# The w_up products of a decoder layer in Strassen's form, in three passes of 688 tokens

## The chip, the cores and the metric

The kernel runs on one core of a Trainium2 chip. The metric is the device time of one execution in microseconds (us). The core has five engines that run their own instruction streams: TensorE (PE; its weight loads are listed as PEld), VectorE (DVE), ScalarE (ACT), GpSimd (POOL) and SyncE (SP), which issues most of the DMA transfers. SBUF is the working memory of 128 partitions, PSUM the memory that TensorE accumulates in, DRAM the memory off the core.

## The reference

One decoder layer on 2048 prompt tokens and 8 single-token samples, 2056 rows in all, of width 1024. Attention (dilated windows) and retention run side by side; their outputs go through `w_out`. The part that is changed follows:

```python
x1  = layernorm(ALPHA * x + mix, ln1_g, ln1_b)
h   = jnp.square(jax.nn.relu(jnp.einsum('btd,df->btf', x1, w_up)))   # 1024 -> 4096
ffn = jnp.einsum('btf,fd->btd', h, w_down)                           # 4096 -> 1024
y   = layernorm(ALPHA * x1 + ffn, ln2_g, ln2_b)
```

All inputs and outputs are float32.

## The kernel before

Every matrix product is made from two parts of each operand: a high part, rounded to the type that TensorE reads at full pace (`split`: ScalarE makes `h`, VectorE the rest `l = raw - h`), and three products, `wh*xh + wh*xl + wl*xh` (`gemm`, lines 244 to 246). One matmul takes a 128x128 block of weights and up to 512 columns of tokens. Activations lie with the model dimension on the partitions and the tokens along the columns.

The kernel has two halves. In the first, four quarters of 512 tokens go through the input projection, attention, retention and the output projection `w_out`; its `evac_out` writes `ALPHA*x + mix` to DRAM (`zd`). In the second, the feed-forward part (`ffn(s)`), two passes `s` take 1024 and 1032 tokens. A pass walks over 8 groups `g`. In a group, four tiles `f` of `w_up` (each 128 output columns, K = 1024 in 8 steps) give four tiles of the hidden layer: `up` accumulates 24 matmuls for each chunk of tokens in a PSUM bank (`ups`), ScalarE makes relu (`rl`) and its square's high part (`hid`), GpSimd the square in float32, VectorE the low part. Then four tiles of `w_down`, of 1024 columns, give eight outputs: `down` accumulates 12 matmuls per chunk (`dps`), and VectorE adds the bank to `ya`, which holds the pass's result in SBUF over all groups. Pass 0 uses two chunks of 512 tokens, pass 1 three of 344, the first and last groups other cuts (`w_keep` holds four weights and walks over chunks outside).

Weights come one at a time from `wseq` (`w_load`: 512 KB into `wr`, on SP; `w_split`: `wh`, `wl`, three buffers each). `fx` holds x1 of the pass, high and low parts.

LN1 is a stream of jobs (`ln_jobs`: sums, mean by a matmul with ones `lm`, centring, sum of squares, `lvv`, scale and shift), one for each chunk of 344 tokens, in slots that own temporaries. `tick(pe)` advances a planned time as products are emitted and emits jobs of the streams whose engines are planned to be free within 4 us; `flush` emits the rest of them without products between. The compiler's list scheduler then sets each engine's order from priorities (program order) and readiness. LN1 of pass 0 starts while `w_out` of the last quarters still runs; the first group of pass 0 takes its first chunk when that chunk's LN is done. LN1 of pass 1 runs during pass 0, goes to DRAM as two parts (`xd`), and in the last group of pass 0 is loaded to `fx` by DMAs on GpSimd's queue. LN2 (`ln_out`) of a pass follows its last group; for pass 1 the centring is done ahead, with weights of the last group shifted by their mean (`w_mean`).

Of the kernel before, what the change touches and what calls it, by code (L numbers as in the profile page):

```python
# [17 lines left out]
P = 128  # L18
# [3 lines left out]
NB = 8  # L22
# [20 lines left out]
TA = -0.2  # L43
CEN_P = (1, 5)
# [14 lines left out]
class Trunk:  # L59
# [105 lines left out]
    def w_split(self, k):  # L165
        if k in self.wraw:
            nc = self.nc
            if k in self.wkeep:
                h, l = self.pa.tile([P, 2, 1024], F32R, tag="zc0", name=f"wk{k}").rearrange("p a c -> a p c")
            else:  # L170
                h = self.wp.tile([P, 1024], F32R, tag="wh", name=f"wh{k}", bufs=3)
                l = self.wp.tile([P, 1024], F32R, tag="wl", name=f"wl{k}", bufs=3)
# [3 lines left out]
            for c in range(0, 1024, 256 if k == 0 else 1024):  # L176
                c = slice(c, c + (256 if k == 0 else 1024))
                if k not in self.wcen:
                    self.split(h[:, c], l[:, c], w[:, c], "s", "v")
            if k in self.wcen:  # L180
# [5 lines left out]
            if self.at is None:  # L186
                self.busy(A=0.95, D=1.13)
            self.wrdy[k] = (h, l)

    def w_mean(self, g):  # L190

        nc = self.nc
        t = self.pa.tile([P, KT, FC], F32, tag="zc1", name="wm").rearrange("p a b -> p (a b)")
# [8 lines left out]

    def w_next(self):
        k = self.wpos
        self.wpos += 1
        if self.whold is None:
            self.w_load(k + 3)
            self.wdue = k + 2
            if self.at is not None:
                self.w_split(k + 1)  # L210
        else:
            self.whold.append(k)
        self.w_split(k)
        return self.wrdy.pop(k)

    def w_keep(self, n):

        ws = []
        for c in range(n):
            for f in range(4):  # L220
                if c == 0:
                    if f == 2:
                        self.whold = []
                    ws.append(self.w_next())
                yield c, f, ws[f]
                if c == n - 1 and f < 2:
                    k = self.whold[f]
                    self.w_load(k + 3)
                    self.w_split(k + 2)
        self.wdue = self.wpos + 1  # L230
        self.whold = None
# [27 lines left out]
    def x_load(self, src, smp):  # L259

        if self.xpre is not None:
            while len(self.loads) > 3:
                self.load_step()
# [737 lines left out]
    def ln_begin(self):  # L1001
        self.streams, self.loads, self.vt = [], [], 0.0
        self.tf = dict(D=0.0, A=0.0, P=0.0, T=0.0, Q=0.0)
# [54 lines left out]
    def ln_jobs(self, z, n, gi, slot, out=None, fin=None, part="all", c=None, last=False):  # L1058
# [63 lines left out]
        def app(k):  # L1122
# [15 lines left out]
            if 0 <= k - 2 < KT:  # L1138
                ops.append(("A", A * (2 if k - 2 in app_p and gi == 0 else 1), 0))
            if 0 <= k - 4 < KT and gi == 0:  # L1140
                ops.append(("P", G, 0) if k - 4 in app_p else ("D", D, 0))
# [25 lines left out]
    def run(self):  # L1167
# [19 lines left out]
        self.wkeep = set()  # L1187
        for s in range(2):
            for g in range(8):
                if s == 0 and g == 0:  # L1190
                    self.wkeep.add(len(wseq) + 3)
                if g == 7:
                    self.wkeep.add(len(wseq) + 7)
                    self.wcen = range(len(wseq) + 4, len(wseq) + 8)
                wseq += [i["w_up"][4 * g + f] for f in range(4)]
                wseq += [i["w_down"][g, d] for d in range(4)]

# [5 lines left out]
        self.whold = None  # L1203
# [18 lines left out]
        self.zd = [self.dram(f"zd{s}", [P, KT, 1024 + NB * s]) for s in range(2)]  # L1222
# [46 lines left out]
        def evac_out(j):  # L1269
            def f(m, c0, n, ps):  # L1270
                np_ = min(n, TQ - c0)
                s, base = divmod(j * TQ, 1024)
# [5 lines left out]
                if c0 + np_ == TQ:  # L1278
                    nc.sync.dma_start(self.zd[s][:, m, base:base + TQ], self.z[m][:, :TQ])
                if np_ < n:  # L1280
                    nc.vector.scalar_tensor_tensor(out=self.z[m][:, TQ:], in0=self.xs[:, m, :], scalar=ALPHA,
                                                   in1=ps[:, np_:n], op0=OP.mult, op1=OP.add)
                    nc.sync.dma_start(self.zd[1][:, m, 1024:], self.z[m][:, TQ:])
# [31 lines left out]
        self.hp = self.ctx.enter_context(tc.tile_pool(name="hp", bufs=4, side="right"))  # L1315
        for s in range(2):
            self.ffn(s)
# [23 lines left out]
    def ffn_open(self):  # L1341
# [8 lines left out]
        self.slots = [dict(pool=self.pa, id=k) for k in range(2)]  # L1350
        self.fx = self.ffn_x()
        ch = self.ffn_chunks(0)
        self.lnx = [self.ln_in(0, 0, *ch[0])]
# [7 lines left out]
        self.lnx.append(self.ln_in(0, 1, *ch[1]))  # L1361

    def tz_open(self):
# [3 lines left out]
        self.slots.append(dict(pool=self.tz, id=2))  # L1367
        self.lnx.append(self.ln_in(0, 2, *self.ffn_chunks(0)[2]))
# [21 lines left out]
    def ffn_chunks(self, s):  # L1390
        return [(0, FC), (FC, FC), (2 * FC, 1024 + NB * s - 2 * FC)]

    def ffn_x(self):
        return [[self.pa.tile([P, 1024 + NB], F32R, tag=f"fx{p}", name=self.nm("fx"), bufs=KT) for p in range(2)]
                for _ in range(KT)]

    def ln_in(self, s, k, c0, n):

        nc = self.nc
        slot = self.slots[k]  # L1400
        t = slot["pool"].tile([P, KT, FC], F32, tag=f"zc{k}", name=self.nm("zc"))
        z = [t[:, k, :n] for k in range(KT)]
        hs = {}

        def load(k):
            nc.sync.dma_start(t[:, k:k + 4, :n], self.zd[s][:, k:k + 4, c0:c0 + n])

        def out(k, g, b):
            h = hs[k] = self.fx[k][0][:, c0:c0 + n] if s == 0 else self.ln_tmp(slot, "lsq", n)
            if k in APP_P:  # L1410
                nc.scalar.activation(z[k], z[k], AF.Identity, bias=b, scale=g)
                nc.scalar.activation(h, z[k], AF.Copy)
            else:
                nc.scalar.activation(h, z[k], AF.Identity, bias=b)

        def fin(k, b):
            h = hs.pop(k)
            l = self.fx[k][1][:, c0:c0 + n] if s == 0 else z[k]
            if k in APP_P:
                nc.gpsimd.tensor_tensor(out=l, in0=z[k], in1=f32(h), op=OP.subtract)  # L1420
            else:
                nc.vector.scalar_tensor_tensor(out=l, in0=z[k], scalar=b, in1=f32(h), op0=OP.add, op1=OP.subtract)  # L1422
            if s == 1:
                nc.sync.dma_start(self.xd[0][:, k, c0:c0 + n], f32(h))
                nc.sync.dma_start(self.xd[1][:, k, c0:c0 + n], l)

        st = self.stream(self.ln_jobs(z, n, 0, slot, out, fin), slot["id"], 1e9)

        def ready():
            st["ends"] = [self.vt + 4.0] * 3  # L1430

        self.loads += [(lambda k=k: load(k), 3.2) for k in (0, 4)] + [(ready, 0.0)]
        return st

    def ln_out(self, s, ya, k, c0, n, sq=None, last=False):
# [8 lines left out]
        def fin(k, b):  # L1444
            ks = slice(k if last else k - 1, k + 1)
            if k % 2 or last:
                self.nc.sync.dma_start(self.o["y"][:, ks, 1024 * s + c0:1024 * s + c0 + n], ya[:, ks, c0:c0 + n])
# [3 lines left out]

    def ffn(self, s):
        nc = self.nc
# [244 lines left out]
```

## Time and profile before

| | us |
|---|---|
| median of 3 runs (2710.18 to 2712.81) | 2710.77 |
| the profiled execution | 2711.21 |
| its span in the profile | 2709.2 |
| TensorE busy | 2650.6 |
| VectorE busy | 1458.1 |
| ScalarE busy | 958.3 |
| GpSimd busy | 633.8 |

The profile names each instruction by its line, its engine, and out<-in by tile. A page gives busy times, then the span cut into 40 slices with a digit each (9 is 90% or more). Groups of instructions show count, busy us, mean ns of one, and the idle time of the engine before them with what ended it. A row of the table by stretches reads: stretch and its length, then busy us (and count) of PE, PEld, DVE, ACT, POOL, then the clock that TensorE was granted (1 is full), the share of the DMA engines and GB/s. Rows of a tile show count, shortest / median / longest ns, first and last start. Times within the profile are us from the span's start. Matmuls overlap, so the spacing of their starts is their cost, not the duration of one.

### The profile page before, as it was taken

The page shows a single profiled execution, that of the slowest core. Times are in us where ns is not written, and L with a number is a line of the kernel's source. Part 1 is how long each engine was busy: PE and PEld are TensorE (multiplying, and loading weights), DVE is VectorE, ACT ScalarE, POOL GpSimd, SP SyncE. Part 2 cuts the span into 40 slices and gives each one's busy share as a digit, 9 for nine tenths or more (in the row PEclk, how much of TensorE's full clock was granted, in tenths as well). Part 3 has the DMA queues.
Part 4 walks back from the last instruction along what each step waited for, and adds up shares of the span by engine and source line. Part 5 has one row for each costly group of instructions (what it writes and reads, how often), then busy time and mean ns, then how long its engine had stood idle before and what let it go on. Part 6 is the DMA issues. An engine that isn't in the chain of part 4 may idle for free.

```text
span 2709.2 us, 41044 instructions
## 1 busy us (share of the span) xinstructions
PE 2650.6 (98%) x16084; PEld 2338.0 (86%) x16084; DVE 1458.1 (54%) x2752; ACT 958.3 (35%) x1940; POOL 633.8 (23%) x598
## 2 busy tenths in 40 slices
PE   8999999999999999989999999999999999999998
PEld 7998788767777888878888888888999999999998
DVE  4667876656676666668544535323574332233366
ACT  3445445344443544435132313221252122212225
POOL 2123543312232122245121302110441001101132
PEclk8999999999999999999999999999999999999999
DMA  7345764755656444472213311211431111111112
GB/s 239 125 126 172 219 195 148 224 188 162 188 180 220 156 149 137 146 253 93 74 53 114 110 47 60 76 47 47 172 109 47 47 47 47 47 46 45 47 44 71
DMA packets 166996, 319.56 MB, mean 118 GB/s; under 512 B 27745, under 2 KB 82722, under 8 KB 166259
## 3 DMA queue, kind: packets, MB, share of 16 engines
q1 hardware_dynamic: 157796, 291.09, 33.6%
q0 software_dynamic: 5760, 21.04, 2.4%
q10 hardware_dynamic: 3248, 4.82, 0.5%
q8 instruction: 126, 2.06, 0.3%
q14 instruction: 66, 0.54, 0.1%
HBM read 256.76 MB, written 60.13 MB: 117 GB/s over the span
## 4 chain that ended last, share of the span: by engine, by line
PE 83%; DVE 6%; DMA 5%; issue 2%; POOL 2%; ACT 1%; SPq 0%; DVEq 0%; POOLq 0%; ACTq 0%
PE dps L246 9%; PE dps L245 9%; PE dps L244 9%; PE ups L246 8%; PE ups L245 8%; PE ups L244 8%; PE gps L244 6%; PE gps L246 5%; PE gps L245 5%; PE o L591 3%; PE ptps L560 2%; PE vps L345 2%; PE vps L347 2%; PE vps L346 2%; PE sps L534 1%
## 5 line engine op out<-in xcount | busy, mean ns | idle before, releaser
L252 ACT ACTIVATE wh<-wr 128x1024 fp32r<-128x1024 f32 (+1 forms) x269 | 281.0, 1047 | 771.2 <-PE dps L245 449.8
L257 DVE TENSOR_TENSOR wl<-wr,wh 128x1024 fp32r<-128x1024 f32 (+1 forms) x269 | 339.9, 1266 | 211.1 <-ACT wh L252 206.7
L245 PE MATMUL ups<-fx,wh 128*128 128x344 f32 (+2 forms) x1288 | 446.1, 346 | 4.4 <-DVE fx L1422 4.4
L246 PE MATMUL ups<-fx,wl 128*128 128x344 f32 (+2 forms) x1288 | 446.5, 347 | 0.2 <-DVE wl L257 0.2
L244 PE MATMUL ups<-fx,wh 128*128 128x344 f32 (+2 forms) x1288 | 445.2, 346 | 0.0
L246 PE MATMUL dps<-hid,wl 128*128 128x344 f32 (+4 forms) x1288 | 441.1, 344 | 0.0
L245 PE MATMUL dps<-hid,wh 128*128 128x344 f32 (+4 forms) x1288 | 440.0, 343 | 0.0
L244 PE MATMUL dps<-hid,wh 128*128 128x344 f32 (+4 forms) x1288 | 436.7, 341 | 0.0
L244 PE MATMUL gps<-xh,wh 128*128 128x512 f32 (+2 forms) x1120 | 400.8, 360 | 9.8 <-ACT xh L252 9.8
L245 PE MATMUL gps<-xl,wh 128*128 128x512 f32 (+2 forms) x1120 | 399.4, 357 | 4.9 <-POOL xl L257 2.9
L246 PE MATMUL gps<-xh,wl 128*128 128x512 f32 (+2 forms) x1120 | 399.1, 357 | 2.2 <-DVE wl L257 2.2
L1473 POOL TENSOR_TENSOR rl<-rl 128x344 f32<-128x344 f32 (+2 forms) x164 | 150.8, 920 | 952.8 <-ACT hid L1472 950.4
L1490 DVE TENSOR_TENSOR ya<-dps,ya 128x344 f32<-128x344 f32 (+4 forms) x296 | 164.9, 560 | 289.3 <-PE dps L246 288.9
L245 PEld LDWEIGHTS ups<-fx,wh 128*128 128x128 f32 x1288 | 242.8, 188 | 27.1 <-DVE fx L1422 6.2
L1474 DVE TENSOR_TENSOR hid<-rl,hid 128x344 fp32r<-128x344 f32 (+2 forms) x164 | 98.2, 600 | 302.2 <-POOL rl L1473 302.2
L246 PEld LDWEIGHTS ups<-fx,wl 128*128 128x128 f32 x1288 | 242.6, 188 | 20.1 <-DVE wl L257 0.5
L244 PEld LDWEIGHTS ups<-fx,wh 128*128 128x128 f32 x1288 | 242.8, 188 | 19.8
L245 PEld LDWEIGHTS dps<-hid,wh 128*128 128x128 f32 x1288 | 241.8, 188 | 20.0
L244 PEld LDWEIGHTS dps<-hid,wh 128*128 128x128 f32 x1288 | 242.0, 188 | 19.4
L246 PEld LDWEIGHTS dps<-hid,wl 128*128 128x128 f32 x1288 | 241.8, 188 | 18.9
L244 PEld LDWEIGHTS gps<-xh,wh 128*128 128x128 f32 x1120 | 213.5, 191 | 47.4 <-ACT xh L252 12.3
L245 PEld LDWEIGHTS gps<-xl,wh 128*128 128x128 f32 x1120 | 214.0, 191 | 41.7 <-issue 7.0
(252 smaller groups left out, 4104.5 us busy)
## 6 DMA issues: line engine op xcount, KB each, us to landing
wr<-in_w_in SPq DMA_DIRECT2D x111, 512.0 KB
wr<-in_w_up SPq DMA_DIRECT2D x64, 512.0 KB
wr<-in_w_down SPq DMA_DIRECT2D x64, 512.0 KB
xr<-in_x SPq DMA_DIRECT2D x64, 256.0 KB
wr<-in_w_out SPq DMA_DIRECT2D x32, 512.0 KB
fx<-xd POOLq DMA_DIRECT2D x16, 516.0 KB, 10.1
t<-modd SPq DMA_DIRECT2D x16, 512.0 KB
ab<-ad SPq DMA_DIRECT2D x32, 256.0 KB
```

What stands on the lines that cost most here:

```text
L244: mm(ps, wh, xh[:, c0:c0 + n], start=(k == 0), stop=False)
L245: mm(ps, wh, xl[:, c0:c0 + n], start=False, stop=False)
L246: mm(ps, wl, xh[:, c0:c0 + n], start=False, stop=(k == last))
L252: nc.scalar.activation(h, raw, AF.Copy)
L257: (nc.vector if eng_l == "v" else nc.gpsimd).tensor_tensor(out=l, in0=raw, in1=f32(h), op=OP.subtract)
L345: mm(o, xh[:, t], wh, start=(k == 0), stop=False)
L346: mm(o, xh[:, t], wl, start=False, stop=False)
L347: mm(o, xl[:, t], wh, start=False, stop=(k == KT - 1))
L591: nc.tensor.matmul(out, v, s["PT"][x][:, col + k * P:col + (k + 1) * P], start=(k == 0), stop=(k == nk - 1))
L1473: nc.gpsimd.tensor_tensor(out=r, in0=r, in1=r, op=OP.mult)
L1474: late.append(lambda: nc.vector.tensor_tensor(out=l, in0=r, in1=f32(h), op=OP.subtract))
L1490: nc.vector.tensor_tensor(out=y, in0=ps, in1=y, op=OP.add)
```

## The change

The up products are made in Strassen's form with seven block products (Winograd's variant), the passes become three, and everything that feeds them is rewritten.

- **Products.** A *set* (`up_set`) is a pair of `w_up` tiles, both halves of K (512 each) and both halves of the pass's tokens. `product` accumulates 12 matmuls of one block (4 K steps, 3 part products). Four PSUM banks X, Y, Z, W take seven products; X, Z and W are added to twice, the second time after another engine has read the first. A group has two sets.
- **Sums of weight blocks.** `f_prep` makes the seven left operands of a set: three are blocks as loaded, four come from four subtractions and additions of 128x512 on GpSimd. Each operand is split as before, ScalarE and VectorE, 512 columns a piece, up to four products ahead.
- **Sums of token blocks.** `build` makes the seven right operands from LN1's result, which now goes to DRAM whole (`x1d`) and is read back in two halves through one buffer; per K step four differences (two on GpSimd, two on VectorE) and seven splits. For pass 0 this runs between `w_out` and the first product; for passes 1 and 2 during the pass before, to DRAM (`xd`, 14 tensors), loaded in group 7 by GpSimd's queue.
- **Passes.** Three of 688, 688 and 680 tokens, in halves of 344, 344, 340; all weights are read and split three times. `ya` starts as x1, loaded from `x1d` at the start of the pass on GpSimd's queue; y of passes 0 and 1 goes to DRAM (`yd`) in group 7, and LN2 runs on it in the next pass. One slot for LN instead of two or three. In the last group the chunks are 340, 170 and 170.

```diff
+PW = 688
+NPASS = 3
+WIDTH = (344, 344, 340)
+ORD = ("B11", "T2", "B21", "T3", "T1", "T4", "B22")
...
+    def f_prep(self, q):
...
+        elif j == 1:
+            z["t"] = self.up.tile([P, 512], F32, tag="ft", name=self.nm("ft"), bufs=1)
+            pl(out=z["t"], in0=z["a11"], in1=z["a21"], op=OP.subtract)
+            pl(out=z["a21"], in0=z["a21"], in1=z["a22"], op=OP.add)
+            pl(out=z["a11"], in0=z["a21"], in1=z["a11"], op=OP.subtract)
+            src = z["a11"]
+            self.busy(P=3.9)
...
+        else:
+            pl(out=z["a12"], in0=z["a12"], in1=z["a11"], op=OP.subtract)
+            src = z["a12"]
...
+        t = self.wp.tile([P, 2, 512], F32R, tag="wh" if self.fpar else "wl", name=self.nm("fu"), bufs=3)
+        self.split(t[:, 0], t[:, 1], src, "s", "v")
...
+    def build_jobs(self, s, slot, t, i, kt, n, D, A, G):
...
+        return [diff("P", t3, d, b), part("B11", a, 1), diff("P", b, b, a), part("B22", d, 1), part("T3", t3, 0),
+                diff("D", d, d, b), part("B21", c, 1), diff("D", c, c, d), part("T1", b, 0), part("T2", d, 0),
+                part("T4", c, 0)]
...
+    def product(self, ps, x, n, start, stop):
+        mm = self.nc.tensor.matmul
+        h, l = self.f_next()
+        xh, xl = x
+        for k in range(4):
+            wh, wl = h[:, k * P:(k + 1) * P], l[:, k * P:(k + 1) * P]
+            mm(ps, wh, xh[:, k, :n], start=start and k == 0, stop=False, skip_group_check=not start)
+            mm(ps, wh, xl[:, k, :n], start=False, stop=False, skip_group_check=not start)
+            mm(ps, wl, xh[:, k, :n], start=False, stop=k == 3, skip_group_check=not start)
...
+    def act(self, hid, c, n, r):
+        nc.scalar.activation(h, r, AF.Square)
+        nc.gpsimd.tensor_tensor(out=r, in0=r, in1=r, op=OP.mult)
+        nc.vector.tensor_tensor(out=l, in0=r, in1=f32(h), op=OP.subtract)
...
+    def up_set(self, hid, n):
+        X, Y, Z, W = (self.acc("ups", n) for _ in range(4))
...
+        def cell(f, c, ps, u):
+            r = tmp("rl", 5)
+            if u is not None:
+                nc.vector.tensor_tensor(out=r, in0=u, in1=ps, op=OP.add)
+            nc.scalar.activation(r, ps if u is None else r, AF.Relu)
+            self.act(hid[f], c, n, r)
+        self.product(X, fx["B11"], n, True, True)
+        p1 = tmp("p1")
+        nc.scalar.copy(p1, X)
+        self.product(Y, fx["T2"], n, True, True)
+        u2 = tmp("u2")
+        nc.vector.tensor_tensor(out=u2, in0=p1, in1=Y, op=OP.add)
+        self.product(X, fx["B21"], n, False, True)
+        cell(0, 0, X, None)
+        self.product(Z, fx["T3"], n, True, True)
+        u3 = tmp("u3")
+        nc.vector.tensor_tensor(out=u3, in0=u2, in1=Z, op=OP.add)
+        self.product(W, fx["T1"], n, True, True)
+        cell(1, 1, W, u3)
+        self.product(Z, fx["T4"], n, False, True)
+        cell(1, 0, Z, u2)
+        self.product(W, fx["B22"], n, False, True)
+        cell(0, 1, W, u2)
...
+    def ffn_all(self):
+        self.f_open()
+        self.flush(self.streams)
+        self.build(0, self.slots[0])
+        self.flush(self.streams)
...
     def ffn(self, s):
...
+        for c in range(2):
+            nc.gpsimd.dma_start(self.ya[:, :, c * n:(c + 1) * n], self.x1d[s][:, c])
+        if s:
+            for c in range(2):
+                self.ln2(s - 1, c, self.slots[0])
+        if not last:
+            for c in range(2):
+                self.ln1(s + 1, c, self.slots[0])
+            self.build(s + 1, self.slots[0])
         for g in range(8):
...
+            for i in (0, 2):
+                self.up_set(hid[i:i + 2], n)
...
+            if g == 7 and not last:
                 self.flush(self.streams)
                 self.fx = self.ffn_x()
+                pend = [(self.fx[o][p][:, :, :WIDTH[s + 1]], self.xd[s + 1, o, p]) for o in ORD for p in range(2)]
...
+                            if g == 7:
+                                nc.sync.dma_start(self.yd[s][:, c, d, :], self.ya[:, d, c * n:(c + 1) * n])
```

More of the change, by code (lines that the diff above doesn't have):

```diff
@@ L1221, in run @@
         self.prologue_late()
[L1222 removed]
+        self.zd = [self.dram(f"zd{s}", [P, KT, PW]) for s in range(NPASS)]
         def evac_in(j):
@@ new lines, in ln2, with out, fin, build @@
+    def ln2(self, s, c, slot):
+        nc, n = self.nc, WIDTH[s]
+        def out(z, k, g, b):
+            nc.scalar.activation(z[k], z[k], AF.Identity, bias=b, scale=g)
+        def fin(t, k):
+            if k % 2:
+                nc.sync.dma_start(self.o["y"][:, k - 1:k + 1, PW * s + c * n:PW * s + (c + 1) * n], t[:, k - 1:k + 1, :n])
+                self.busy(Q=1.5)
+        self.stream(self.ln_z(s, c, slot, 1, self.yd[s][:, c], out, fin), slot["id"], 0.5)
+    def build(self, s, slot):
+        nc, n = self.nc, WIDTH[s]
+        D, A, G = n * 1.04e-3 + 0.15, n * 0.84e-3 + 0.2, n * 2.2e-3 + 0.18
+        jobs = []
+        for q in range(2):
+            def srcs(q=q):
+                x = self.x1d[s]
+                return [(2 * b, 2 * b + 2, x[:, c, 4 * h + 2 * q:4 * h + 2 * q + 2, :])
+                        for b, (c, h) in enumerate(((0, 0), (0, 1), (1, 0), (1, 1)))]
+            t, first = self.begin(slot, srcs)
+            jobs.append(first)
+            for i in range(2):
+                jobs += self.build_jobs(s, slot, t, i, 2 * q + i, n, D, A, G)
+        return self.stream(jobs, slot["id"], 0.5)
@@ new lines, in down @@
+    def down(self, hid, g, u, dd, d, c0, n, sq=None, slot=0):
+        nc = self.nc
+        ps = self.acc("dps", n)
+        a, b = (x.rearrange("p (f d) -> p f d", f=4) for x in u)
+        mm = nc.tensor.matmul
+        for k in range(4):
+            wh, wl = a[:, k, dd * P:(dd + 1) * P], b[:, k, dd * P:(dd + 1) * P]
+            xh, xl = (x[:, c0:c0 + n] for x in hid[k])
+            mm(ps, wh, xh, start=(k == 0), stop=False)
+            mm(ps, wh, xl, start=False, stop=False)
+            mm(ps, wl, xh, start=False, stop=(k == 3))
+            if k == 1:
+                self.tick(n * 2.75e-3)
+        y = self.ya[:, d, c0:c0 + n]
+        if g == 0:
+            nc.vector.scalar_tensor_tensor(out=y, in0=y, scalar=ALPHA, in1=ps, op0=OP.mult, op1=OP.add)
+        else:
+            nc.vector.tensor_tensor(out=y, in0=ps, in1=y, op=OP.add)
+        if sq is not None:
+            sq[d] = f32(self.ln_tmp(self.slots[slot], "lsq", n))
+            with self.tc.high_priority(offset=SP):
+                nc.scalar.activation(sq[d], y, AF.Square)
+                if d >= 2:
+                    (nc.vector if d % 2 or d == 6 else nc.gpsimd).tensor_tensor(out=sq[d], in0=sq[d], in1=sq[d - 2],
+                                                                                op=OP.add)
+            self.busy(A=0.3, D=0.2, P=0.35)
+        self.tick(n * 2.75e-3, D=0.51)
@@ L1535, in ffn @@
+            if g < 7 or not last:
                 for dp in range(4):
[L1536 removed]
+                    u = self.f_next()
                     for dd in range(2):
[L1538 to L1558 removed]
@@ new lines, in ffn @@
+            if g == 6 and last:
+                z = [self.ya[:, d, :n] for d in range(KT)]
+                for c in range(2):
+                    z = [self.ya[:, d, c * n:(c + 1) * n] for d in range(KT)]
+                    self.stream(self.ln_jobs(z, n, 1, self.slots[0], part="cen"), 0, 0.7)
+                self.f_mean(7)
+            if g == 7 and last:
+                self.flush(self.streams)
+                us = [self.f_next() for _ in range(4)]
+                cs = [(0, n), (n, n // 2), (n + n // 2, n // 2)]
+                for c, (c0, m) in enumerate(cs):
+                    sq = {}
+                    for dp in range(4):
+                        for dd in range(2):
+                            self.down(hid, g, us[dp], dd, 2 * dp + dd, c0, m, sq, 0)
+                    self.ln_out(s, self.ya, 0, c0, m, sq, c == len(cs) - 1)
```

397 lines of the change are left out of this document (199 added, 198 removed).

## Prediction

> **What bounds the kernel now.** I read the page first: the span, the busy times, and the 40 slices.
>
> ```profile
> span 2709.2 us, 41044 instructions
> PE 2650.6 (98%) x16084; PEld 2338.0 (86%) x16084; DVE 1458.1 (54%) x2752; ACT 958.3 (35%) x1940; POOL 633.8 (23%) x598
> ...
> PE   8999999999999999989999999999999999999998
> PEld 7998788767777888878888888888999999999998
> DVE  4667876656676666668544535323574332233366
> ...
> GB/s 239 125 126 172 219 195 148 224 188 162 188 180 220 156 149 137 146 253 93 74 53 114 110 47 60 76 47 47 172 109 47 47 47 47 47 46 45 47 44 71
> ```
>
> TensorE is busy 98% of the span; the second half, the feed-forward part, is the flattest of it. But busy time there is a modelled end, so I take the pace from periods: in the chain of waits, the first down product of a group comes round again after one group of four w_up tiles.
>
> ```profile
> 1650.00 0.46 PE dps L244 x2
> ...
> 1739.69 0.46 PE dps L244 x2
> ...
> 1828.75 0.46 PE dps L244 x2
> ...
> 2110.18 0.32 PE dps L244 x2
> ...
> 2200.86 0.31 PE dps L244 x2
> ...
> 2692.30 0.42 DVE ya L1490
> ```
>
> In pass 0 a group is 192 up and 192 down matmuls of 512 columns: 1828.75 - 1739.69 = 89.06, or 231.9 ns each. In pass 1 it is 288 and 288 of 344 columns: 2200.86 - 2110.18 = 90.68, or 157.4 ns each. The table by stretches gives the same and the rate at 256 to 264 columns: 40 / 337 = 118.7 ns, a slope of 0.45 ns a column.
>
> ```profile
> 2020.00:2600.00 580.00, 580.00 (x3685) 580.00 (x3684) 194.96 (x314) 119.85 (x195) 62.61 (x76) 1.00 0.14 47
> ```
>
> ```profile
> 2650.00:2690.00 40.00, 40.00 (x337) 40.00 (x337) 27.20 (x62) 22.81 (x56) 8.78 (x11) 1.00 0.16 54
> ```
>
> The first up product and the waits of TensorE from there on:
>
> ```profile
> L244 PEld LDWEIGHTS ups<-fx,wh x1288: 187/188/331, 1234.3 to 2649.2; 128*128 128x128 f32 x184
> ```
>
> ```profile
> PE lvv L1117 <- ACT lsq L252: 5.6, 3, 3.0
> PE ups L245 <- DVE fx L1422: 4.4, 4, 2.9
> ```
>
> So the feed-forward part lasts from 1234.3 to 2692.3, 1458.0, nearly without a wait. What shortens or interrupts TensorE's stream there moves the end one for one.
>
> **The change, part by part.**
>
> *Products removed and narrowed.* A set of Strassen's form takes 7 block products of 12 matmuls for a pair of w_up tiles and two halves of the tokens, where 8 were. A group is 2 x 84 up and 192 down matmuls, 360 of 344 columns. Passes 0 and 1: 2 x 8 x 360 x 157.4 = 906.6. Pass 2 at 340 columns, 155.6 ns: 7 x 360 x 155.6 = 392.1, in its last group 264 x 155.6 = 41.1, and 192 matmuls of 170 columns; those are narrower than any here, so I carry the slope on: 79.1 ns, 15.2 (between 77.8 ns, half of a 340-column one, and 118.7, no gain below 256: 14.9 to 22.8). Together 1355.0, against 1458.0: 103 less if nothing waits. All else is to be taken from this.
>
> *The start of the feed-forward part.* Before, up products begin on the first third of pass 0 as soon as its LN is done, and the other two chunks follow beside them. Afterwards the program finishes both LN chunks, writes x1 to DRAM, reads it back, and makes seven sums and their high and low parts for four pieces of K, in two halves through one buffer. The first product needs a piece of all four. Nothing covers this: w_out has ended.
>
> ```profile
> 1193.79 0.94 SPq L1406 DMA_DIRECT2D zc<-zd  x2
> ...
> 1259.02 0.93 SPq L1406 DMA_DIRECT2D zc<-zd  x2
> ```
>
> ```profile
> 1223.40 2.21 DVE L1100 TENSOR_TENSOR zc<-zc,lm 128x344 f32<-128x344 f32 x5
> ...
> 1256.27 2.68 DVE L1422 SCALAR_TENSOR_TENSOR fx<-zc,lnp,fx 128x344 fp32r<-128x344 f32 x4
> ...
> 1263.43 0.52 DVE L1075 TENSOR_TENSOR lsq<-zc 128x344 f32<-128x344 f32 x1 [1.60 <-DMA zc<-zd]
> ```
>
> The second chunk is centred from 1223.4 and its last part ends at 1259.0, with the third chunk's LN and the splits beside it, which go. I take 1245 (1238 to 1259). A load takes 4.4 from issue to first use (1259.02 to 1263.43); write and read back 7 (5 to 8): 1252. A K piece is 9 VectorE operations of 0.52 to 0.56 (rows below) and two GpSimd ones, which delay some: a half 11.5 (10 to 14), 1263.5. The second half's load waits for the buffer: 5.5, 1269. The last piece's second operand is there after another 10.5, 1279.5, when 3.4 of products are already done: as if dense from 1276, 42 after 1234.3 (30 to 63). The weights' splits hide in the load's waits; without that, two of 0.69.
>
> *Seven splits, sums and cells in a set.* Per set TensorE takes 84 x 157.4 = 13.2. The other engines, by the rows of the same shapes:
>
> ```profile
> L1490 DVE TENSOR_TENSOR ya<-dps,ya 128x344 f32<-128x344 f32 x160 | 81.8, 515 | 162.2 <-PE dps L246 162.2
> L1473 POOL TENSOR_TENSOR rl<-rl 128x344 f32<-128x344 f32 x96 | 81.0, 844 | 526.4 <-ACT hid L1472 526.2
> L1474 DVE TENSOR_TENSOR hid<-rl,hid 128x344 fp32r<-128x344 f32 x96 | 53.4, 557 | 170.2 <-POOL rl L1473 170.2
> ...
> L1472 ACT ACTIVATE hid<-rl 128x344 fp32r<-128x344 f32 x96 | 47.1, 491 | 2.8
> L1471 ACT ACTIVATE rl<-ups 128x344 f32<-128x344 f32 x96 | 43.4, 452 | 131.0 <-PE ups L246 130.9
> L1473 POOL TENSOR_TENSOR rl<-rl 128x512 f32<-128x512 f32 x40 | 41.7, 1043 | 300.9 <-ACT hid L1472 298.7 <-DVE hid L1474 2.1
> L1474 DVE TENSOR_TENSOR hid<-rl,hid 128x512 fp32r<-128x512 f32 x40 | 27.8, 694 | 96.1 <-POOL rl L1473 96.1
> L1472 ACT ACTIVATE hid<-rl 128x512 fp32r<-128x512 f32 x40 | 25.3, 633 | 1.3
> ```
>
> VectorE: 7 x 0.694 + 5 x 0.515 + 4 x 0.557 = 9.7. ScalarE: 7 x 0.633 + 5 x 0.452 + 4 x 0.491 = 8.7. GpSimd: 4 x 1.043 + 4 x 0.844 = 7.5. None exceeds 13.2, and in the down part (30.2 a group) VectorE has 16 x 0.515 + 4 x 1.23 = 13.2 and GpSimd nothing. So throughput holds; new are short waits. X may be added to again only when ScalarE has copied p1, Z when VectorE has made u3, W when it has made the cell's sum: each has one product, 1.89, for at most one instruction ahead (0.69) and its own 0.52. That fits. After the last product the cell's chain (0.52, 0.45, 0.49, 0.84, 0.56, one behind the other: 2.9 with nothing between) meets the down product of the second half after 3.0: I give 0.2 a group, 5 in all (0 to 20).
>
> *LN and build beside the products.* LN of the next pass, LN2 of the last one and build now run in up sets whose VectorE is 73% full. Eight chunks of some 23 VectorE operations of 0.6 and two builds of 36 of 0.55 are 150; a group of 56.7 leaves VectorE 56.7 - 2 x 9.7 - 13.2 = 24.1, so they lie over some 6 to 7 groups, 14 of the 48 sets. Between 1175 and 1200, where VectorE was about as full, TensorE lost a quarter; between 1210 and 1230, nothing.
>
> ```profile
> 1175.00:1200.00 25.00, 19.14 (x87) 14.78 (x86) 20.20 (x27) 9.85 (x18) 15.73 (x11) 0.93 0.75 250
> ...
> 1210.00:1220.00 10.00, 10.00 (x46) 8.18 (x45) 9.17 (x14) 8.44 (x16) 4.81 (x4) 1.00 0.69 217
> 1220.00:1230.00 10.00, 10.00 (x45) 8.07 (x44) 10.00 (x15) 3.45 (x7) 4.05 (x4) 1.00 0.21 77
> ```
>
> Over these 45 it lost 5.9, 13%; I take 9%, since part of that loss was the next block's first operands, which these sets already hold: 14 x 13.2 x 0.09 = 16 (0 to 43, the quarter). LN's own matmuls and the clock after the start's gap (0.93 above): 6.
>
> *Pass changes.* 14 loads of 704 KB (9.9 MB) are to land behind group 7's up sets, beside 2.8 MB of y writes and some 2 MB of weights: 14.7 MB in 30.2 of down products, 487 GB/s. The most that a stretch moved is 332:
>
> ```profile
> 1920.00:1940.00 20.00, 20.00 (x128) 20.00 (x128) 10.35 (x21) 0.49 (x1) 6.75 (x9) 1.00 0.91 332
> ```
>
> At 332 it takes 44, and the last operand is wanted after 30.2 + 11.3 = 41.5: 3 late, and a wait in GpSimd's queue, where the ya loads stand behind the last y write, with the set's own sums and squares queued behind them: 2 more. Two changes, 10 (0 to 30). The third reading of the weights is 33.5 MB more at a mean of 47 to 74 GB/s, prefetched four deep: nothing, and if the prefetch fails some 3 a set.
>
> *Last group.* Its centring, mean of w_down and LN fall on two up sets (26) instead of four tiles (45), and the tail's LN has one slot for two: 8 (4 to 20). The extra pieces of zd writes, and the xd, x1 and y writes of SP, wait for nobody that TensorE waits for: nothing.
>
> Sum: 1355 + 42 + 5 + 16 + 6 + 10 + 8 = 1442, 16 less than 1458. The profiled execution took 2711.2 (span 2709.2, 2.0 around it; the median of the runs, 2710.77, is 0.4 below): **2695**.
>
> **A rule that speaks against it.** VectorE's operation on two SBUF tensors was sometimes twice as long; the one that reads PSUM and one SBUF tensor never:
>
> ```profile
> L1474 DVE TENSOR_TENSOR hid<-rl,hid x135: 501/518/1234, 1522.2 to 2648.1; 128x344 fp32r<-128x344 f32 x95, 128x512 fp32r<-128x512 f32 x40
> ```
>
> ```profile
> L1490 DVE TENSOR_TENSOR ya<-dps,ya x238: 492/517/693, 1501.7 to 2604.7; 128x344 f32<-128x344 f32 x80, 128x512 f32<-128x512 f32 x35, 128x336 f32<-128x336 f32 x4
> ```
>
> 1234 - 518 = 716 ns is nearly a GpSimd operation. If the two exclude each other, a set needs 7.5 of GpSimd and 7 x 0.694 + 4 x 0.557 = 7.1 of VectorE one after the other, 14.6, over its 13.2. The Trainium skill states this (SBUF — State Buffer, section "SBUF: two separate sides"): the port pair that the two share is an exclusive lock for a whole instruction; the trace's 501 against 1234 ns agrees. I still take no loss per set, since four splits and three sums of a group (5.9) can be made in the down part before it, and some 2.8 falls behind it: 29.2 - 8.7 = 20.5 in 26.4.
>
> **Rivals.**
> - *The port decides* (slower). Each set takes 14.6 instead of 13.2: 48 x 1.4 = 67 in place of the 5: 2757. For it: the sum of the rows; against: buffers reach ahead. It turns the sign from 16 / 48, 0.33 a set.
> - *The waits hide.* Start 30, LN 5, changes and cells nothing, last group 4, LN's matmuls 6: 1400, **2653**. For it: from 1300 to 1916 TensorE shows no wait at all.
> - *The start is longer.* LN's second chunk ends as late as now and the halves take 14: 42 becomes 58: 2711, no change.
>
> **How the numbers follow.** Forecast 0.46 (its own range 2680 to 2710), hidden waits 0.20, port 0.22, longer start 0.12. 2650 to 2740 leaves out most of the port's case at its full price, and the ends beyond. Faster by over 0.2% (5.4, about what a measurement can tell) is the second case and most of the first: 0.61; within it 0.12; slower, the port's case and a part of the start's: 0.27.
>
> **What would show it.** After: no up product before about 1270, and TensorE idle 30 to 45 there, with build's splits on VectorE; groups of 56.7 in the quiet parts (over 58 says port or cells); waits of ups on VectorE and ScalarE of under 1 each; at the two pass changes ups waiting for fx loads; 170-column matmuls near 79 ns. I am wrong if a quiet group is longer than 58, or if the start gap passes 60.

## The result, and the profile after

| | us |
|---|---|
| before, median of 4 runs (2706.33 to 2712.81) | 2710.47 |
| after, median of 4 runs (2727.12 to 2735.42) | 2730.89 |
| ratio, with its 95% interval | 1.0078 [1.0057, 1.0099] |
| the profiled execution of after, its span | 2727.12, 2725.3 |

The changed kernel is slower by 0.8%, where 2695 was forecast. The products did become cheaper by nearly the 103 us; that went elsewhere, and 16 to 20 more (the profiled execution is the lowest of the four). The first lines and five of the 40-slice lines of its page:

```profile
span 2725.3 us, 44939 instructions
...
PE 2613.6 (96%) x16852; PEld 2403.9 (88%) x16852; DVE 1868.4 (69%) x3411; ACT 1176.5 (43%) x2420; POOL 972.2 (36%) x849
...
PE   8999999999999999996999999999999999999998
...
DVE  4667876556776666667886655688875568756567
...
POOL 2123533322331122335543233555542345333342
PEclk8999999999999999997999999999999999999999
```

TensorE's busy time fell only from 2650.6 to 2613.6, VectorE's rose by 410 and GpSimd's by 338. The heaviest places of VectorE in the second half (788, 8887, 87) are those of GpSimd (554, 5554, 53 in the same slices). The feed-forward part runs from the first `ups` weight load to the last addition to `ya`:

```profile
L1589 PEld LDWEIGHTS ups<-fx,fu x1344: 186/188/338, 1229.5 to 2678.6; 128*128 128x128 f32 x192
```

```profile
L1657 DVE TENSOR_TENSOR ya<-dps,ya x344: 317/512/519, 1375.8 to 2714.5; 128x344 f32<-128x344 f32 x112, 128x340 f32<-128x340 f32 x52, 128x170 f32<-128x170 f32 x8
```

So 1485.0 us instead of 1458.0, 27.0 longer. `w_out` ended 4.8 earlier, and what follows the last addition took 10.8 (2725.3 - 2714.5) instead of 16.9, 6.1 less: 27.0 - 4.8 - 6.1 = 16.1, the difference of the spans. The table by stretches tells where the 27 lie:

```profile
1229.60:1282.00 52.40, 25.23 (x94) 20.78 (x93) 39.00 (x57) 24.03 (x51) 27.47 (x22) 0.64 0.57 198
1282.00:1450.00 168.00, 154.83 (x909) 150.24 (x908) 141.30 (x213) 81.90 (x160) 79.49 (x69) 0.94 0.50 170
1450.00:1710.00 260.00, 260.00 (x1651) 259.94 (x1650) 153.86 (x239) 96.51 (x168) 88.96 (x78) 1.00 0.24 77
1710.00:1760.00 50.00, 48.98 (x309) 48.42 (x308) 30.84 (x46) 14.82 (x26) 21.53 (x26) 1.00 0.92 337
1760.00:2020.00 260.00, 246.56 (x1482) 241.22 (x1481) 226.24 (x332) 132.07 (x261) 136.53 (x114) 0.96 0.48 161
2020.00:2200.00 180.00, 180.00 (x1144) 180.00 (x1143) 109.86 (x169) 68.23 (x120) 66.12 (x61) 1.00 0.29 91
2200.00:2240.00 40.00, 37.90 (x230) 37.18 (x230) 21.01 (x33) 9.01 (x15) 14.23 (x15) 0.96 1.11 323
2240.00:2360.00 120.00, 109.98 (x676) 107.42 (x675) 101.17 (x147) 56.67 (x110) 58.92 (x52) 0.97 0.46 152
```

Read each row as length minus 157.4 ns for each matmul: that is what the stretch lost. 1450 to 1710 and 2020 to 2200 lost nothing (260 - 1651 x 0.1574 = 0.1): the bare Strassen groups, with seven splits, four sums and four cells a set, are fully hidden. In 1282 to 1450, 1760 to 2020 and 2240 to 2360 run LN and `build` beside the products; there VectorE goes from 59% to 84 to 87% busy, GpSimd from 34% to 47 to 53%, and 24.9, 26.7 and 13.6 are lost, 65.2 in all. (From 2240 on the matmuls are 340 wide and cost 155.6 ns; by that the last of the three is 14.8, the figure in the expectations below.) Of the 65.2, 36.6 are idle TensorE (length minus its busy time). The other 28.6 lie in its busy time, and the lower clock (0.94, 0.96, 0.97) makes some 24 of them: 168 x 0.06 + 260 x 0.04 + 120 x 0.03.

How such a loss comes about, in the timeline of TensorE, VectorE and GpSimd (start, duration, what it is, in brackets the idle time before it and what ended it):

```profile
1298.95 0.32 PE L1650 MATMUL dps<-hid,fl 128*128 128x344 f32 x1
1302.21 0.62 PE L1648 MATMUL dps<-hid,fh 128*128 128x344 f32 x1 [2.94 <-DVE rl L1613]
```

```profile
1296.45 5.18 DVE L1180 TENSOR_TENSOR zc<-zc,lm 128x344 f32<-128x344 f32 x6
1301.56 0.92 DVE L1613 TENSOR_TENSOR rl<-u,ups 128x344 f32<-128x344 f32 x2
```

```profile
1295.22 2.09 POOL L1180 TENSOR_TENSOR zc<-zc,lm 128x344 f32<-128x344 f32 x2
1297.96 1.31 POOL L276 TENSOR_TENSOR ft<-fr,fr 128x512 f32<-128x512 f32 x1 [0.64 <-DMA fr<-in_w_up]
1300.24 1.02 POOL L1176 TENSOR_TENSOR lsq<-lsq,lsq 128x344 f32<-128x344 f32 x1 [0.97 <-ACT lsq L1183]
```

Six centrings of LN take 5.18 on VectorE, 0.86 each, while GpSimd centres, sums weights and adds squares. Behind them in VectorE's queue stand the cell's additions, which free the banks that the down products need; TensorE stands for 2.94. And then the clock:

```profile
1299.00:1302.20 3.20, 0.27 (x2) 0.03 (x1) 3.20 (x6) 0.60 (x2) 2.23 (x3) 0.99 0.00 0
1302.20:1305.60 3.40, 3.39 (x12) 3.40 (x13) 3.30 (x4) 2.44 (x6) 2.66 (x4) 0.51 0.19 41
1305.60:1309.00 3.40, 3.40 (x23) 3.32 (x22) 3.40 (x7) 0.98 (x2) 1.93 (x2) 1.00 0.30 118
```

After the gap the clock is 0.51 for 3.4 us: 12 matmuls where the next 3.4 us hold 23. This gap of 2.94 costs some 4.6 (11 matmuls of 0.157 on top). The largest waits of TensorE over the span (us in total, times, longest):

```profile
PE ups L1589 <- ACT fx L332: 21.4, 2, 16.9
PE dps L1648 <- DVE rl L1613: 12.2, 4, 3.8
PE dps L1649 <- DVE hid L1602: 9.0, 10, 2.1
```

The first is the gap at the start; the others are down products that wait for VectorE.

What VectorE and GpSimd took in the feed-forward part (groups by line and shape: count, busy us, mean ns of one, idle time before):

```profile
L337 DVE TENSOR_TENSOR fu<-fr,fu 128x512 fp32r<-128x512 f32 x287 | 222.7, 789 | 50.2 <-ACT fu L332 49.2
...
L1602 DVE TENSOR_TENSOR hid<-rl,hid 128x344 fp32r<-128x344 f32 x128 | 101.9, 800 | 31.1 <-POOL rl L1601 31.1
L290 POOL TENSOR_TENSOR fr<-fr 128x512 f32<-128x512 f32 x48 | 77.3, 1610 | 125.6 <-DVE fu L337 125.6
L276 POOL TENSOR_TENSOR ft<-fr,fr 128x512 f32<-128x512 f32 x48 | 68.2, 1420 | 52.7 <-DMA fr<-in_w_up 47.3 <-DVE fu L337 5.4
...
L1613 DVE TENSOR_TENSOR rl<-u,ups 128x344 f32<-128x344 f32 x96 | 48.6, 507 | 34.0 <-PE ups L1591 33.9
...
L1180 DVE TENSOR_TENSOR zc<-zc,lm 128x344 f32<-128x344 f32 x36 | 32.1, 956 | 0.0
```

Splits take 789 instead of the 694 that I took, the hidden layer's low parts 800 instead of 557, GpSimd's sums 1420 and 1610 instead of the 1043 that I took from its squares. The addition with an operand in PSUM (L1613) takes 507, as ever.

The single operations of this trace, by their starts and ends, say what these means are made of. Of the 192 low parts, 107 ran while GpSimd made no operation: 509 ns on the mean, 519 at most. The 82 with GpSimd busy for at least 30% of their length took 1167. The additions with a PSUM operand took 505 and 506 in the same two cases. So VectorE's operations on two SBUF tensors are longer only where GpSimd works, and one with a PSUM operand isn't touched. Of GpSimd's 192 sums, the 74 during which VectorE had no operation on SBUF tensors alone took 1290 (median), the others 1540: the meeting makes these longer too, but most of the step from 1043 is that a sum reads two blocks and a square one.

### The profile page after: what moved, and what is told of

It reads as the page before. It is cut to its first block, busy times and chain, and to the rows that moved or that the text cites. A ratio compares the mean times of both kernels' runs of the same rounds, so it can differ in the third digit from the quotient of the medians.

```text
span 2725.3 us, 44939 instructions
## 1 busy us (share of the span) xinstructions
PE 2613.6 (96%) x16852; PEld 2403.9 (88%) x16852; DVE 1868.4 (69%) x3411; ACT 1176.5 (43%) x2420; POOL 972.2 (36%) x849
## 5 line engine op out<-in xcount | busy, mean ns | idle before, releaser
L1649 PE MATMUL dps<-hid,fh 128*128 128x344 f32 (+2 forms) x1544 | 496.3, 324 | 9.1 <-DVE hid L1602 9.0
L1650 PE MATMUL dps<-hid,fl 128*128 128x344 f32 (+2 forms) x1544 | 493.4, 323 | 3.2 <-DVE fl L337 3.1
L1648 PE MATMUL dps<-hid,fh 128*128 128x344 f32 (+2 forms) x1544 | 478.5, 324 | 17.6 <-DVE rl L1613 12.2
L1589 PE MATMUL ups<-fx,fu 128*128 128x344 f32 (+1 forms) x1344 | 435.4, 325 | 29.0 <-ACT fx L332 21.4
L1590 PE MATMUL ups<-fx,fu 128*128 128x344 f32 (+1 forms) x1344 | 435.4, 324 | 3.8 <-DVE fx L337 3.8
L1591 PE MATMUL ups<-fx,fu 128*128 128x344 f32 (+1 forms) x1344 | 426.4, 323 | 0.8 <-DVE fu L337 0.8
L332 ACT ACTIVATE fu<-fr 128x512 fp32r<-128x512 f32 x288 | 176.2, 627 | 341.5 <-PE dps L1649 250.4
L1648 PEld LDWEIGHTS dps<-hid,fh 128*128 128x128 f32 x1544 | 292.7, 192 | 21.2 <-ACT zc L1505 7.2
L1649 PEld LDWEIGHTS dps<-hid,fh 128*128 128x128 f32 x1544 | 295.6, 192 | 13.1 <-DVE hid L1602 12.9
L1650 PEld LDWEIGHTS dps<-hid,fl 128*128 128x128 f32 x1544 | 296.0, 192 | 5.2 <-DVE fl L337 5.2
L1589 PEld LDWEIGHTS ups<-fx,fu 128*128 128x128 f32 x1344 | 256.7, 191 | 33.1 <-ACT fx L332 22.8
L1601 POOL TENSOR_TENSOR rl<-rl 128x344 f32<-128x344 f32 (+1 forms) x192 | 191.5, 1000 | 222.6 <-ACT hid L1600 222.4
L1590 PEld LDWEIGHTS ups<-fx,fu 128*128 128x128 f32 x1344 | 256.4, 191 | 5.8 <-DVE fx L337 5.5
L337 DVE TENSOR_TENSOR fu<-fr,fu 128x512 fp32r<-128x512 f32 x288 | 223.4, 788 | 51.3 <-ACT fu L332 50.3
L1591 PEld LDWEIGHTS ups<-fx,fu 128*128 128x128 f32 x1344 | 255.4, 191 | 1.5 <-DVE fu L337 1.5
L326 PEld LDWEIGHTS gps<-xh,wl 128*128 128x128 f32 x1120 | 213.5, 191 | 33.3 <-DVE wl L337 3.2
```

Of the source, the lines that this page charges most:

```text
L326: mm(ps, wl, xh[:, c0:c0 + n], start=False, stop=(k == last))
L332: nc.scalar.activation(h, raw, AF.Copy)
L337: (nc.vector if eng_l == "v" else nc.gpsimd).tensor_tensor(out=l, in0=raw, in1=f32(h), op=OP.subtract)
L1589: mm(ps, wh, xh[:, k, :n], start=start and k == 0, stop=False, skip_group_check=not start)
L1590: mm(ps, wh, xl[:, k, :n], start=False, stop=False, skip_group_check=not start)
L1591: mm(ps, wl, xh[:, k, :n], start=False, stop=k == 3, skip_group_check=not start)
```

## The experiments

Theory P says that this exclusion of VectorE and GpSimd is what the changed kernel pays for. Its rivals: S, that the streams of LN and `build` stand in the wrong place, beside the up products; P2, that not the port (the way into SBUF that the prediction's rule has the two engines share) but the order of GpSimd's queue costs the time, where a sum that waits for a split holds the squares behind it; C, that the halved clock after gaps is a cost of its own, above all at the start; V, that VectorE simply has too much to do there. The loss in the table at the end of this section is that of the three stretches 1282 to 1450, 1760 to 2020 and 2200 to 2360 of each profiled execution, again length minus 157.4 ns a matmul.

**No sums.** The four sums on GpSimd are left out (the operands are blocks as loaded; their splits and all products stay).

```diff
-            pl(out=z["t"], in0=z["a11"], in1=z["a21"], op=OP.subtract)
-            pl(out=z["a21"], in0=z["a21"], in1=z["a22"], op=OP.add)
-            pl(out=z["a11"], in0=z["a21"], in1=z["a11"], op=OP.subtract)
+            z["t"] = z["a21"]
...
-            pl(out=z["a12"], in0=z["a12"], in1=z["a11"], op=OP.subtract)
```

> Edit: the four GpSimd sums of weight blocks of every set are left out (its operands are blocks as loaded, so the hidden layer is not the reference's); splits, products, LN and build stay. The changed kernel loses some 66 us against its matmul count in the stretches where LN or build run beside up sets (24.9 + 26.7 + 14.8), half of it idle TensorE, half a halved clock behind the idle. Theory P (the sums fill the memory port that GpSimd shares with VectorE): 4.2 us of GpSimd a set are gone, at least two thirds of the 66 go: 2660 to 2690. Theory S (the streams' VectorE work in up sets is too much, sums or not): less than a third goes: 2708 to 2725.

Measured 2690.34, ratio 0.9918 [0.9896, 0.994]: 40 below the changed kernel, at the upper bound of P's range (2660 to 2690) and far from S's. The means fall to 653 ns (`hid`) and 747 (split). But the loss falls only from 69.4 to 41.0, two fifths, where P asked for two thirds. Some 7 of the 40 come from the start instead, where 141 matmuls were made by 1282 in place of 94.

**Streams only in the down part.** `tick` steps LN and `build` behind down products alone.

```diff
-    def tick(self, pe, **use):
+    def tick(self, pe, hold=False, **use):
         self.vt += pe
         self.busy(**use)
+        if hold:
+            return
...
-        self.tick(n * 2.75e-3)
+        self.tick(n * 2.75e-3, True)
```

> Edit: the same instructions as the changed kernel, but jobs of LN and build are emitted only during down products (up products advance the planned time without stepping the streams). Theory S (the streams late on VectorE at the cells of an up set): the stretches' loss of 66 us falls to 10 to 30: 2675 to 2700, and the waits of the first down products on VectorE's cell sums nearly vanish; the rest is what the flush ahead of group 7 leaves. Theory P (the weight sums fill the shared port in every up set): little change, 2715 to 2735.

Measured 2728.79, 1.0058 [1.0041, 1.0076], within 2.1 of the changed kernel. S falls: the place of the streams is worth next to nothing. (The three stretches lose 59.8 instead of 69.4, but the streams now reach beyond 2020, and 2020 to 2200 loses 7.2.)

**Sums on VectorE.** The same four sums, on the other engine.

```diff
-        pl = nc.gpsimd.tensor_tensor
+        pl = nc.vector.tensor_tensor
```

> Edit: the four sums of weight blocks of a set on VectorE instead of GpSimd. Theory P: GpSimd's 1.04 us each become 0.69 on VectorE and keep nothing out, the two engines together need less time: 2690 to 2715. Theory S (VectorE itself is what is short beside LN and build): 2.8 us more VectorE work a set, 12.4 of 13.2 us: the gaps grow and come to quiet groups too: 2740 to 2800.

Measured 2700.05, 0.9948 [0.993, 0.9965]: faster than before, although VectorE has 192 operations more. One takes 0.72 to 0.85 us there, the four 150 us over the kernel; on GpSimd they held 274.

**Last chunks 340 and 340** instead of 340, 170, 170.

```diff
-                cs = [(0, n), (n, n // 2), (n + n // 2, n // 2)]
+                cs = [(0, n), (n, n)]
```

> Edit: the last group's chunks are 340 and 340 instead of 340, 170 and 170. If a 170-column matmul costs a floor of about 0.111 us (spacing in the changed kernel's trace near the end): 192 x 0.111 = 21.3 become 96 x 0.1556 = 14.9, 6.4 us less TensorE, and the LN tail behind the last product is longer by 5 to 9 us: within 4 us of the changed kernel. If the spacing there was a wait and not a floor: 2733 to 2740, since only the tail's growth is left.

Measured 2729.64, 1.0059 [1.0031, 1.0087], 1.3 from the changed kernel: the narrow matmuls are no gain, since they cost nearly as much as wide ones. The stretch of the 170-column matmuls in the changed kernel:

```profile
2700.00:2712.00 12.00, 12.00 (x110) 12.00 (x110) 9.33 (x23) 7.91 (x20) 4.15 (x6) 1.00 0.33 117
```

12.0 / 110 is 109 ns each (111 between starts), not 79: TensorE and its weight loads are both busy throughout.

**Idle sums.** As the first experiment, but with four subtractions of 128x512 a set on GpSimd whose result nobody reads.

```diff
+            ft = self.up.tile([P, 512], F32, tag="ft", name=self.nm("ft"), bufs=1)
+            for q_ in range(3):
+                pl(out=ft, in0=z["a11"], in1=z["a21"], op=OP.subtract)
...
+            pl(out=ft, in0=z["a12"], in1=z["a22"], op=OP.subtract)
```

> Edit: as e1 (operands are blocks as loaded, the hidden layer is not the reference's), but GpSimd again makes four subtractions of 128x512 a set, into a tile that nobody reads, so that no operand waits for them and they wait for nothing but the weights' load. Theory P1 (the port: each of these keeps VectorE's operations on two SBUF tensors out while it runs): e1's gain goes again for the most part, 2712 to 2735, and VectorE's fu splits and hid subtractions grow from 747 and 653 ns towards 789 and 800. Theory P2 (the queue: the sums in place wait for the splits that still read the blocks, the squares behind them in GpSimd's queue wait along): no wait comes back: 2685 to 2702.

Measured 2739.12, 1.0115 [1.0093, 1.0136]: all that leaving out the sums gave is gone, and 8 more (4 above P1's range; the interval just touches that of the changed kernel), though no operand waits for these operations. One of its stretches, its largest wait of TensorE after the start, and the low part's group:

```profile
1282.00:1450.00 168.00, 144.38 (x841) 139.42 (x840) 142.09 (x203) 77.86 (x155) 83.14 (x70) 0.94 0.50 164
```

```profile
PE dps L1650 <- DVE hid L1603: 29.0, 16, 4.4
```

```profile
L1603 DVE TENSOR_TENSOR hid<-rl,hid 128x344 fp32r<-128x344 f32 x128 | 106.3, 833 | 35.4 <-POOL rl L1602 35.4
```

The low part takes 833 and TensorE waits 29 for it; the split grew only from 747 to 761. What costs is that GpSimd works, not that anyone waits for its sums. A square does still stand behind these operations on GpSimd; that share isn't separated from the port's.

**Sums into tiles of their own** on GpSimd, two buffers each, so that no sum waits for the split of the block that it overwrites.

```diff
-            pl(out=z["a21"], in0=z["a21"], in1=z["a22"], op=OP.add)
-            pl(out=z["a11"], in0=z["a21"], in1=z["a11"], op=OP.subtract)
+            pl(out=z["s21"], in0=z["a21"], in1=z["a22"], op=OP.add)
+            pl(out=z["s11"], in0=z["s21"], in1=z["a11"], op=OP.subtract)
...
-            pl(out=z["a12"], in0=z["a12"], in1=z["a11"], op=OP.subtract)
+            pl(out=z["s12"], in0=z["a12"], in1=z["s11"], op=OP.subtract)
```

> Edit: the sums of weight blocks stay on GpSimd but go to tiles of their own, two buffers each, instead of onto the blocks that splits still read. Theory P2 (queue): the waits of GpSimd in front of the sums (some 270 + 126 us in the changed kernel) shrink, the squares behind them come in time: 2695 to 2712. Theory P1 (port): the same GpSimd work at the same places, 2724 to 2735.

Measured 2761.22, 1.0193 [1.017, 1.0216]: 30 above the changed kernel, and above the ranges of both theories. P2 as stated falls, since the waits for splits at the head of GpSimd's queue went and the time rose. The largest wait of TensorE, the low part's group, and a stretch that was without loss so far:

```profile
PE dps L1651 <- DVE hid L1604: 37.7, 26, 5.9
```

```profile
L1604 DVE TENSOR_TENSOR hid<-rl,hid 128x344 fp32r<-128x344 f32 x128 | 101.4, 795 | 42.5 <-POOL rl L1603 42.5
```

```profile
1450.00:1710.00 260.00, 252.34 (x1570) 249.59 (x1570) 151.37 (x237) 90.83 (x158) 86.03 (x74) 0.99 0.24 78
```

Even the bare groups now lose 12.9. Longer operations aren't the reason: the low part takes 795, as in the changed kernel (800), and GpSimd's squares are shorter (893 ns on the mean, 1000 in the changed kernel). What grew is VectorE's wait for the square (42.5 instead of 31.1). The sums now run back to back, and a square that is ready stands behind them: in 1450 to 1710 it starts 0.96 us after ScalarE's high part on the mean, instead of 0.58. So the order of GpSimd's queue does cost time of its own, if not in the way that P2 said; how the loss of the changed kernel divides between it and the port isn't separated.

**Streams only in the down part, with the sums on VectorE** (both edits above).

> Edit: sums of weight blocks on VectorE (e3) and jobs of LN and build only during down products (e2). Theory S, weakened (with GpSimd relieved, what is left of the loss in the stretches is the place of the streams): 2670 to 2690 against e3's 2700. If their place does not matter, as in e2: 2697 to 2705.

Measured 2692.44, 0.9936 [0.9916, 0.9956], apparently 8 below the sums on VectorE alone. In five more rounds side by side:

> Sums on VectorE and streams stepped only in the down part, in more rounds: if the place of the streams is worth what one comparison of three rounds suggested, 5 to 10 us below the kernel that has only the sums on VectorE; if that was chance, within 3 us of it.

> Sums on VectorE alone, in more rounds beside the kernel with the streams also moved: 2700 again, 5 to 10 us above that one if the place of the streams matters here, within 3 us if not.

2698.87, 0.996 [0.9944, 0.9975], against 2702.76, 0.9965 [0.9952, 0.9978]. The 8 were mostly chance; 4 remain, and the intervals overlap. The place of the streams is again worth next to nothing.

**A warm start.** The sums on VectorE, and 108 matmuls of ones (their bank isn't read) in the gap before the first product.

```diff
+        ps, x = self.bank(self.ps, "warm", 344), self.fx["B11"][0][:, 0, :344]
+        for q_ in range(108):
+            nc.tensor.matmul(ps, self.ones_r, x, start=True, stop=True)
```

> Edit: e3 with 108 matmuls (of ones, read by nobody) ahead of the first product, behind the first piece of build, so that TensorE is busy for the first 17 us of the gap at the start of the feed-forward part. Theory C (the halved clock behind the gap, 34 us long in e3's trace, costs time of its own): products of the first set run at 157 instead of 288 ns: 3 to 9 us less than e3, 2691 to 2697. If data alone paces these products: no difference, 2698 to 2703, or more if the 108 reach past the gap.

Measured 2702.48, 0.9972 [0.9959, 0.9985], nothing gained. The clock of the start stretch did rise, from 0.64 to 0.84:

```profile
1229.60:1282.00 52.40, 42.28 (x216) 38.26 (x215) 39.42 (x68) 24.87 (x52) 17.35 (x14) 0.84 0.58 202
```

The same stretch of the kernel with the sums on VectorE and without them:

```profile
1229.60:1282.00 52.40, 26.36 (x99) 21.43 (x100) 40.09 (x68) 24.75 (x52) 17.92 (x15) 0.64 0.56 198
```

Of the 216 matmuls 108 are the added ones, and the 108 left compare with these 99. The first products are paced by `build`, not by the clock; C falls there. (Beside the streams the lower clock is a real part of the loss, the 24 us above, but as what follows a gap.)

**The port relieved from the other side.** The GpSimd operations of LN and `build` in the feed-forward part go to VectorE, first in the changed kernel (its sums still on GpSimd), then with the sums on VectorE and the streams in the down part.

```diff
+        E = "P"
+        if self.sv and not last:
+            p, E, G = v, "D", D
...
         def diff(eng, out, a, b):
+            eng = "D" if self.sv else eng
...
+        self.sv = True
```

> The changed kernel, with only the GpSimd operations of the LN and build streams of the feed-forward part moved to VectorE (some 100 operations of 128x344 to 128x344: about 90 us less on GpSimd, 55 more on VectorE); the four sums of a set stay on GpSimd. Theory P (the two engines exclude each other, so every GpSimd operation beside the sets costs VectorE its own length): less GpSimd time to be excluded by, 2700 to 2722. Theory V (VectorE simply has too much to do in the stretches with the streams, whoever else works): 55 us more on it make it worse, 2735 to 2765.

> The kernel with the sums on VectorE and the streams stepped only in the down part, and the streams' GpSimd operations on VectorE too: GpSimd keeps the squares alone. Theory P: a little faster than with the streams' share on GpSimd, 2680 to 2692. Theory V: VectorE has the sums, the streams and all else, and is the bound in those stretches: 2697 to 2720.

Measured 2713.55, 1.0009 [0.9998, 1.0019], 17 below the changed kernel, and 2676.11, 0.9877 [0.9862, 0.9891], 23 below the same kernel without this edit and faster than both kernels by more than 1%. V falls twice: more work on VectorE made the kernel faster both times, the second time by 4 more than P's range had it. In the second kernel GpSimd keeps the squares and the issue of some DMAs, and beside them only work of the start and the tail. Its groups and two of its stretches:

```profile
L337 DVE TENSOR_TENSOR fu<-fr,fu 128x512 fp32r<-128x512 f32 x288 | 199.0, 703 | 34.0 <-ACT fu L332 32.9
...
L1608 DVE TENSOR_TENSOR hid<-rl,hid 128x344 fp32r<-128x344 f32 x128 | 76.0, 596 | 21.8 <-POOL rl L1607 21.8
...
L1619 DVE TENSOR_TENSOR rl<-u,ups 128x344 f32<-128x344 f32 x96 | 48.5, 505 | 26.8 <-PE ups L1597 26.6
...
L1185 DVE TENSOR_TENSOR zc<-zc,lm 128x344 f32<-128x344 f32 x48 | 23.3, 553 | 0.0
```

```profile
1282.00:1450.00 168.00, 161.13 (x1003) 159.01 (x1003) 146.99 (x272) 86.36 (x169) 22.96 (x23) 0.99 0.50 170
...
1760.00:2020.00 260.00, 253.48 (x1589) 251.62 (x1589) 218.07 (x409) 132.47 (x254) 37.16 (x35) 0.99 0.42 141
```

The centring is down from 956 to 553 ns, the low part from 800 to 596, the split from 789 to 703; the addition with a PSUM operand stays (507, 505). In 1282 to 1450 VectorE made 272 operations in 147.0 us where it made 213 in 141.3, GpSimd worked 23 instead of 79, and TensorE issued 94 matmuls more.

| kernel | loss in three stretches | span | span - loss |
|---|---|---|---|
| after | 69.4 | 2725.3 | 2655.9 |
| no sums | 41.0 | 2686.6 | 2645.6 |
| idle sums | 89.7 | 2737.8 | 2648.1 |
| sums on VectorE | 47.3 | 2698.1 | 2650.8 |
| streams' share on VectorE | 59.0 | 2710.2 | 2651.2 |
| both, streams in the down part | 19.6 | 2675.7 | 2656.1 |
| streams only in the down part | 59.8 | 2727.1 | 2667.3 |
| sums into tiles of their own | 79.1 | 2759.0 | 2679.9 |

In the first six rows what is left of the span varies by 11 us, the spans by 62: these versions differ mainly in what the three stretches lose. The last two lose in other places as well, above all in the groups named at their experiments (7.2 and 12.9).

## Why the prediction was wrong, point by point

- **Dense products:** right. Quiet groups run at 157.4 ns a matmul without a loss, 56.7 a group, as forecast. Only the 170-column matmuls were off: "I carry the slope on: 79.1 ns, 15.2" should have been 21 (192 x 0.111), near the upper bound of 22.8.
- **Start:** right in size, 42 forecast; 52.4 - 94 x 0.1574 = 37.6 found. Its course was another: six up products ran at 1229.7 and more from 1247.7 on, as their operands came, where none was expected before 1270; TensorE was idle for 27.2 (52.4 - 25.23), not 30 to 45, and the other 10 lie in matmuls at a lower clock (0.64 over the stretch).
- **Sets and cells, 5:** right in the quiet stretches (0.1 in 260). The waits of `ups` on VectorE and ScalarE that I expected there are hidden.
- **LN and build beside the products:** the step that failed. "14 x 13.2 x 0.09 = 16 (0 to 43, the quarter)" was 65.2 in the three stretches, 49 too little, which turns 2695 into a slower kernel. Both factors were small. The three stretches hold 1423 up matmuls, which are 17 sets (84 each), not 14. And a set lost 65.2 / 17 = 3.8, 29% of its 13.2, not 9%. The row 1175 to 1200 had shown a quarter (5.9 of 25). I averaged it with two rows without loss to 13%, and went down to 9% because "part of that loss was the next block's first operands". That row had VectorE and GpSimd both busy too (20.20 and 15.73 of 25), so its loss may well have had this cause; no run took it apart.
- **The rule I noted and priced at nothing:** "I still take no loss per set". The exclusive lock that the Trainium skill describes (SBUF — State Buffer, section "SBUF: two separate sides") is borne out by 956 against 553 ns. My reason for no loss holds in the bare groups, where the sums are made ahead; it fails where LN and `build` fill that slack with VectorE and GpSimd work of their own. The rival had the right mechanism and, by chance, the right sum (67): it is not 1.4 in each of 48 sets but 3.8 in 17 and nothing in 31. (Its turning point was also off: with the 5 for waits taken out, the sign turns at 21 / 48, 0.44 a set.)
- **Lengthened operations as a sum:** I took 694, 557 and 1043 ns from a kernel in which these engines met less often. They were 789, 800 and 1339 to 1610. The last was mispriced from the start: 1043 is a square's, and a sum of two blocks takes 1290 with no such operation of VectorE beside it.
- **Pass changes:** 10 forecast, 2200 to 2240 lost 40 - 230 x 0.1574 = 3.8, and the first one (1710 to 1760) 1.4: 5. The loads did land in time, at 323 and 337 GB/s: no product waited for one.
- **Last group:** 8 forecast, some 5 found beside the narrow matmuls (2360 to 2690: 330 - 2088 x 0.1556); the tail behind it was 6.1 shorter, which no term had.

By these terms: 1355 + 6 (narrow) + 38 + 65 + 5 + 5 + 5 (LN's matmuls) = 1479 of the 1485.0; 6 stay unplaced. The time lies inside the range of 2650 to 2740, through the port's case; the sign was wrong. The two signs that would have told me so, a quiet group over 58 and a start gap over 60, did not show (56.7 and 38): they watched the places where nothing was lost.

## What to carry to other kernels

An engine share of 60 to 70% says nothing of headroom where VectorE and GpSimd work on SBUF tensors at the same time: add their SBUF operations up in the stretch where they meet, as one resource; VectorE's operations with a PSUM operand can run beside GpSimd's. Look also at what stands behind a long operation in GpSimd's queue. Moving work from GpSimd to the busier VectorE can then be the faster choice; here it was, three times. When a row of the old profile shows a loss in a stretch like the one being planned, take its rate whole unless a run shows the other cause.

## What the runs showed of the hardware that I had not expected

- A gap of 2.94 us of TensorE was followed by 3.4 us at clock 0.51, so this wait cost about half as much again. Not every such gap does it: after one of 2.35 us, at 2313, the clock stayed at 1.00. The Trainium skill (TensorE: Matmul & The Clock Gate, "Part 1: The HAM clock gate") gives 3413 ns for the window, which agrees with the 3.4; it puts the return to half clock after an idle window of about that length, while here 2.94 was enough.
- A 170-column matmul with new weights costs 109 to 111 ns, against 118.7 at 256 to 264 columns: below these widths there is nearly nothing to gain.
- GpSimd's sum of two 128x512 blocks took 1.34 to 1.61 us on the mean in the changed kernel, and 1.29 where VectorE had no operation on SBUF tensors alone; VectorE did it in 0.69 to 0.83 when it had the streams' work as well.
